# SSD decay factors on POOL and ACT alone, four factor buffers and the x weight pool at the other end of SBUF

## The chip, the cores and the metric

One core of a Trainium2 chip (trn2) runs the whole program. The metric is the device time of one execution, in microseconds (us). Before the change it is 1627.95 us, the median of three runs (1626.01 to 1629.65).

## The reference, cut to what matters

The network has a first block of two layers and a second block of two: an attention layer and a state-space (SSD) layer, each with a gated feed-forward. It works on 256 tokens of width 1024, with a context of 256 tokens beside them. The change lies in the SSD layer: 32 heads in 8 groups of 4, two chunks of 128 tokens, both directions. Per chunk and direction the reference computes

```
cum = cumsum(dt * A)
decay = exp(where(tri, cum[..., :, None] - cum[..., None, :], -inf))
cb = einsum('bcign,bcjgn->bcgij', Cc, Bc)
y_diag = einsum('bcghij,bcjghp->bcighp', cb[:, :, :, None] * decay, xdt)
```

with `xdt = x * dt`. For each head the kernel therefore needs a 128x128 matrix of factors, `decay * dt`, for the forward and for the backward direction (a lower and an upper triangle), and multiplies it by C and B's product, which is one for a group.

## The kernel before, in words

The dense layers run in fp32 in three products: each weight tile of 128x1024 is fetched by SP (`fetch`, L170), split into a high part `h` on ACT (L181) and a rest `l` on DVE (L182; on POOL for a few), and TensorE adds high times high, low times high and high times low (all recorded at L132). The x weights have a pool of their own, `wx`: three buffers of `raw`, two of `h`, two of `l`. A second pool, `wc`, and a scratch pool, `cx`, serve the context; they stand at the right end of SBUF and are given up (`cst.close()`) before the SSD layer, whose pool `l1` grows into their place from the left.

`x_ssm` loops over the eight groups. A turn does this:

- `project(g)`: four feature tiles (B, C and two of x, for x and the context together, C for x alone) into the two accumulators `pcvx`; each is convolved along the tokens in `conv_silu` (L1254 on ACT, L1255 and L1257 on DVE, which frees the accumulator, then a tanh on ACT, L1259, and L1260 on DVE). Then the gate `sz` (L1313 on ACT, L1314 on DVE), transposes, weighted copies `xc`, and the state `h0` of the context, copied out by ACT (L1330).
- The product of C and B, `pcb`; transposes and weighted copies `xf`; the state `hn`. Then for each chunk c: `GG` is the factor tile `EW[c]` times `pcb` (L1408, DVE), `pyd` its product with x on TensorE, `poff` the part of the earlier state; DVE sums them in `t` (L1417 to L1420) and gates them into `yg` (L1421); ACT squares it for the norm (L1422).
- `rstd`: a scalar step and a power on POOL (L288, L289); then `decays(g + 1)`; then ACT scales `yg` (L1428), TensorE transposes it into `pyt` (L1430), and it is split into `ysH` (ACT, L1434) and `ysL` (DVE, L1435).

`decays(g)` makes `EW` for both chunks, c = 0 and 1, 128x512 each (four heads). POOL makes two masks times dt, `W` and `Wb`, in one buffer each (L1361), and their sum (L1362). SP fetches the rows of cum, spread over all partitions, into `D_`, 128 partitions x 2 directions x 512, two buffers (L1364, 512 KB). POOL subtracts this token's cum from each direction (L1367, twice), DVE takes the min of both directions (L1368), ACT the exponential (L1370), POOL the product with W into `EW` (L1372), two buffers, one for each chunk.

Which order each engine's list has is settled before the run by the framework's planner, which lays the program out on a simulated timeline: an instruction written later may stand earlier in an engine's list if the planner expects it to be ready. On the chip each engine takes its list in order and waits at the head of it. SP's list holds all the weight and row fetches.

After the loop comes the out projection `ssm_w_out` (`pdx`), then the second feed-forward.

Of the kernel before, what the change touches and what calls it, by code (L numbers as in the profile page):

```python
# [8 lines left out]
F32 = mybir.dt.float32  # L9
F32R = mybir.dt.float32r  # L10
BF16 = mybir.dt.bfloat16
AF = mybir.ActivationFunctionType
ALU = mybir.AluOpType
# [12 lines left out]
CTAG = 's'  # L26
FINM = None
WB = 1
CWP = 1
WA = (0, 0)  # L30
DB = 2
XB = 2
PCB = 'cs'
# [4 lines left out]
PHS = 'cm'  # L38
PHX = 'cm'
POF = 'cd'  # L40
EB = 2
TAD = 'V'
LP = (4, 0, 2, 0, 2, 4)
ARAW = 2
# [3 lines left out]
WX = (3, 2)  # L48
WC = (2, 2)
# [42 lines left out]
def build(tc, A):  # L92
    nc = tc.nc
    T, V, S, G, SY = nc.tensor, nc.vector, nc.scalar, nc.gpsimd, nc.sync
    es = ExitStack()
# [5 lines left out]
    def dram(a, off, ap):  # L101
        return bass.AP(tensor=a.tensor, offset=a.offset + off, ap=ap)

    def pool(name, bufs=1, space=None, right=False):
        kw = {"side": "right"} if right else {}
        if space is not None:
            kw["space"] = space
        else:
            kw["reuse_waits"] = "tile"
        return tc.tile_pool(name=name, bufs=bufs, **kw)  # L110
# [5 lines left out]
    class Banks:  # L116
        def __init__(self, name, bufs):
            self.p = es.enter_context(pool(name, 1, PS))
            self.bufs = bufs
            self.k = name[2]  # L120
# [33 lines left out]
    flip = misc[:, 420:548]  # L154

    class Weights:
        def __init__(self, name, raw, hl, eng, right=False):
            self.p = (cst if right else es).enter_context(pool("w" + name, raw, right=right))
            self.hl = hl
            self.eng = eng  # L160

            self.ahead = []
            self.n = 0
            self.name = name
            self.on_pool = 0
# [21 lines left out]
    def cols(a, ncols, n0, k0=0, kt=8):  # L187
        return [(lambda t: t, dram(a, k0 * 128 * ncols + n0, [[ncols, 128], [128 * ncols, kt], [1, 128]]))]

    wx = Weights("x", *WX, SY)  # L190
    cst = ExitStack()
    wc = Weights("c", *WC, SY, right=True)
    cx = cst.enter_context(pool("cx", right=True))
    xw = es.enter_context(pool("xw"))
    xpool = {"x": (xw, "xn"), "c": (cx, "cfl")}
# [1066 lines left out]
    def heads(ap, n=4, d=64):  # L1262
        return ap[:, :, None].to_broadcast([128, n, d])
# [24 lines left out]
    def x_ssm():  # L1288
        with ExitStack() as st:
# [58 lines left out]
            wst = p.tile([128, 2, 32], F32, name="wst")  # L1348
            for c in range(2):
                V.tensor_tensor(wst[:, c], dec[:, 4 + c], dt[:, c, 32 * c:32 * c + 32], op=ALU.mult)  # L1350
            def decays(g):
                out = []
                for c in range(2):
                    W, Wb = (p.tile([128, 4, 128], F32, tag=n, bufs=WB, name=n) for n in ("W", "Wb"))
                    for d, msk, to in ((0, m_le, W), (1, m_ge, Wb)):
                        j = 32 * d + 4 * g
                        if WA[d]:
                            for h in range(4):
                                S.activation(to[:, h], msk, AF.Copy, scale=dt[:, c, j + h:j + h + 1])
                        else:  # L1360
                            G.tensor_tensor(to, msk[:, None, :].to_broadcast([128, 4, 128]), heads(dt[:, c, j:j + 4], 4, 128), op=ALU.mult)  # L1361
                    G.tensor_tensor(W, W, Wb, op=ALU.add)  # L1362
                    D_ = p.tile([128, 2, 4, 128], F32, tag="D_", bufs=DB, name="D_")
                    SY.dma_start(D_.rearrange("p d h i -> p d (h i)"),  # L1364
                                 dram(cum_s, (2 * c * 32 + 4 * g) * 128, [[0, 128], [32 * 128, 2], [1, 512]]))
                    for d in range(2):
                        G.tensor_tensor(D_[:, d], D_[:, d], heads(cum[:, 2 * c + d, 4 * g:4 * g + 4], 4, 128), op=ALU.subtract)  # L1367
                    V.tensor_tensor(D_[:, 0], D_[:, 0], D_[:, 1], op=ALU.min)  # L1368
                    E = D_[:, 0]
                    S.activation(E, E, AF.Exp)  # L1370
                    EW = p.tile([128, 4, 128], F32, tag="EW", bufs=EB, name="EW")
                    (G if CWP else V).tensor_tensor(EW, E, W, op=ALU.mult)  # L1372
                    out.append(EW)
                return out

            ew = decays(0)
            for g in range(8):
                h0, fT, fC, sz = project(g)
                h4 = slice(4 * g, 4 * g + 4)
                EW = ew  # L1380
                BT, CT = fT[:, 2, 0], fC[:, 0]
                xf = [p.tile([128, 3, 256], F32, tag="xf", bufs=XB, name="xf") for _ in range(2)]
                pcb = PT(PCB).tile([128, 2, 256], F32, tag=PCB[1], name="pcb")
                for c in range(2):
                    cs = slice(c * 128, (c + 1) * 128)
                    mm(pcb[:, c, 0:128], BT[:, cs], CT[:, cs], True, True)
                bt = p.tile([128, 2, 128], F32, tag="bt", bufs=2)
                for c in range(2):
                    cs = slice(c * 128, (c + 1) * 128)
                    pt = PT(PXT).tile([128, 512], F32, tag=PXT[1], name="pxt")  # L1390
                    for i in range(3):
                        T.transpose(pt[:, i * 128:(i + 1) * 128], fT[:, i, 0, cs], ident)
                    S.activation(bt[:, c], pt[:, 256:384], AF.Copy)
                    S.activation(xf[c][:, 0], pt[:, 0:256], AF.Copy)
                    for k, sc in ((2, wst[:, c, h4]), (1, d_row[:, h4])):
                        V.tensor_tensor(hview(xf[c][:, k]), hview(pt[:, 0:256]), heads(sc), op=ALU.mult)
                hn = p.tile([128, 2, 256], F32, tag="hn", bufs=2)
                ph = PT(PHX).tile([128, 2, 256], F32, tag=PHX[1], name="phx")
                for d in range(2):
                    mm(ph[:, d], bt[:, d], xf[d][:, 2], True, True)  # L1400
                    V.tensor_tensor(hview(hn[:, d]), hview(h0[:, d]), heads(dec[:, 6 + d, h4]), op=ALU.mult)
                V.tensor_tensor(hn, hn, ph, op=ALU.add)
                yg = p.tile([128, 2, 256], F32, tag="yg", bufs=2)
                ss = p.tile([128, 2], F32, tag="yss", bufs=2)
                for c in range(2):
                    cs = slice(c * 128, (c + 1) * 128)
                    GG = p.tile([128, 4, 128], F32, tag="GG", bufs=2)
                    V.tensor_tensor(GG, EW[c], pcb[:, c, None, 0:128].to_broadcast([128, 4, 128]), op=ALU.mult)  # L1408
                    py = PT(PYD).tile([128, 512], F32, tag=PYD[1], name="pyd")
                    for h in range(4):  # L1410
                        mm(py[:, h * 64:(h + 1) * 64], GG[:, h], xf[c][:, 0, h * 64:(h + 1) * 64], True, True)
                    po = PT(POF).tile([128, 2, 256], F32, tag=POF[1], name="poff")
                    mm(po[:, 0], CT[:, cs], h0[:, 0] if c == 0 else hn[:, 0], True, True)
                    mm(po[:, 1], CT[:, cs], h0[:, 1] if c == 1 else hn[:, 1], True, True)
                    t = p.tile([128, 2, 256], F32, tag="yt", bufs=1)
                    for d in range(2):
                        V.tensor_tensor(hview(t[:, d]), hview(po[:, d]), heads(dec[:, 2 * c + d, h4]), op=ALU.mult)  # L1417
                    (V if TAD == "V" else G).tensor_tensor(t[:, 0], t[:, 0], t[:, 1], op=ALU.add)
                    (V if TAD == "V" else G).tensor_tensor(t[:, 0], t[:, 0], xf[c][:, 1], op=ALU.add)
                    V.tensor_tensor(t[:, 0], t[:, 0], py[:, 0:256], op=ALU.add)  # L1420
                    V.tensor_tensor(yg[:, c], t[:, 0], sz[:, c], op=ALU.mult)  # L1421
                    S.activation(t[:, 1], yg[:, c], AF.Square, accum_out=ss[:, c:c + 1])  # L1422
                r = rstd(ss, 1024, 2, "y")
                if g < 7:
                    ew = decays(g + 1)
                pt = PT(PYT).tile([128, 2, 2, 128], F32, tag=PYT[1], name="pyt")
                for c in range(2):
                    S.activation(yg[:, c], yg[:, c], AF.Copy, scale=r[:, c:c + 1])  # L1428
                    for k in range(2):
                        T.transpose(pt[:, k, c], yg[:, c, k * 128:(k + 1) * 128], ident)  # L1430
                for k in range(2):
                    kk_ = 2 * g + k
                    pk = pt[:, k].rearrange("p c t -> p (c t)")
                    S.activation(yH[:, kk_], pk, AF.Identity, scale=g_ssm[:, kk_:kk_ + 1])  # L1434
                    V.scalar_tensor_tensor(yL[:, kk_], pk, g_ssm[:, kk_:kk_ + 1], yH[:, kk_].bitcast(F32),  # L1435
                                           op0=ALU.mult, op1=ALU.subtract)
# [71 lines left out]
```

## Time and profile before

| | us |
|---|---|
| three runs | 1626.01, 1627.95, 1629.65 |
| the profiled execution, its own time | 1627.45 |
| its span, first to last instruction | 1625.4 |
| TensorE (PE) busy | 1524.9 |
| VectorE (DVE) busy | 1104.7 |
| ScalarE (ACT) busy | 745.3 |
| GpSimd (POOL) busy | 301.8 |
| loop over the groups, first `sz` of group 0 to first `sz` of group 7 | 1091.0 to 1361.0 |

A span is cut into windows by the reader; a window's line gives each engine's busy time in it, the mean granted clock of TensorE (1.00 is full speed) and the share of its DMA engines that moved data. Rows of the timeline are single instructions: start, length, engine, line of the kernel, and in brackets how long the engine was idle before it and what ended that. The chain of waits follows the end of the program back to what released each step; rows of it are start, length and what. A tile's name may carry a number (`D__12148`): one allocation of it.

### The profile page before, as it was taken

What the parts mean: (1) busy time and instruction counts of PE and PEld (TensorE: products, weight loads), DVE (VectorE), ACT (ScalarE), POOL (GpSimd) and SP (SyncE); (2) the same over time, 40 slices, a digit from 0 to 9 for tenths busy, and PEclk for the clock granted to TensorE, in tenths of its full rate; (3) what the DMA queues carried; (4) which work ended last, traced back from release to release, by engine and by line L of the source; (5) the groups of instructions that cost most, each with busy time, mean ns of one, the idle gap of its engine ahead of it and who ended that gap; (6) DMA issues with size and microseconds to landing.
All of it is one profiled execution on the core that took longest, in us unless ns stands there. A gap on an engine that the chain in (4) does not pass through costs nothing.

```text
span 1625.4 us, 27122 instructions
## 1 busy us (share of the span) xinstructions
PE 1524.9 (94%) x10660; PEld 1307.0 (80%) x10660; DVE 1104.7 (68%) x1823; ACT 745.3 (46%) x1336; POOL 301.8 (19%) x260
## 2 busy tenths in 40 slices
PE   6989987999999999999999999887999999899998
PEld 5655664786998988888889897787899889699997
DVE  6789776567766676655666565569888787655666
ACT  3412256545544544666444343433454444444443
POOL 4476420000100100000000000129454430100000
PEclk9989998999999999999999999889999999999999
DMA  8755574466656656423665766334444433555664
GB/s 264 216 183 170 167 202 138 124 179 209 185 178 205 197 175 194 138 79 95 200 206 183 235 185 204 99 90 131 106 119 117 113 97 114 162 162 176 192 185 136
DMA packets 302735, 264.58 MB, mean 163 GB/s; under 512 B 27329, under 2 KB 256495, under 8 KB 302608
## 3 DMA queue, kind: packets, MB, share of 16 engines
q1 hardware_dynamic: 301680, 259.70, 53.5%
q0 software_dynamic: 928, 3.15, 0.7%
q8 instruction: 84, 1.38, 0.3%
q14 instruction: 43, 0.35, 0.1%
HBM read 261.47 MB, written 1.34 MB: 162 GB/s over the span
## 4 chain that ended last, share of the span: by engine, by line
PE 77%; DVE 7%; DMA 7%; POOL 5%; issue 2%; ACT 1%; SPq 1%; POOLq 0%; DVEq 0%; ACTq 0%
PE pdx L132 21%; PE pffnx L132 16%; PE pffnc L132 8%; PE pdc L132 7%; PE pcvx L132 6%; PE pada L905 3%; DMA araw<-ada_w 2%; PE pg L132 2%; PE py L132 2%; PE pl0x L132 1%; POOL EW L1372 1%; PE pl1x L132 1%; PE pocx L132 1%; PE ptcx L1086 1%; DVE l L182 1%
## 5 line engine op out<-in xcount | busy, mean ns | idle before, releaser
L182 DVE TENSOR_TENSOR l<-raw,h 128x1024 fp32r<-128x1024 f32 (+2 forms) x362 | 452.9, 1254 | 284.8 <-ACT h L181 231.1
L181 ACT ACTIVATE h<-raw 128x1024 fp32r<-128x1024 f32 (+2 forms) x374 | 389.2, 1042 | 487.3 <-PE pdx L132 147.5
L132 PE MATMUL pffnx<-nhx,h 128*128 128x256 f32 x704 | 174.9, 286 | 0.0
L132 PE MATMUL pffnx<-nlx,h 128*128 128x256 f32 x704 | 174.7, 285 | 0.2 <-DVE nlx L352 0.2
L132 PEld LDWEIGHTS pffnx<-nhx,h 128*128 128x128 f32 x704 | 136.5, 194 | 1.2 <-issue 1.2
L132 PEld LDWEIGHTS pffnx<-nlx,h 128*128 128x128 f32 x704 | 136.3, 194 | 1.0 <-DVE nlx L352 0.9
L310 POOL TENSOR_TENSOR sums<-sums,nhalf 128x1 f32<-128x1 f32 x20 | 14.6, 730 | 559.0 <-DVE sums L306 542.0
L132 PE MATMUL pffnx<-nhx,l 128*128 128x256 f32 x704 | 99.0, 283 | 0.0
L905 PE MATMUL pada<-araw,cT 128*32 128x256 f32 x704 | 76.3, 403 | 18.5 <-DMA araw<-ada_w 18.5
L132 PEld LDWEIGHTS pffnx<-nhx,l 128*128 128x128 f32 x704 | 91.1, 193 | 0.0
L132 PE MATMUL pffnc<-nhc,h 128*128 128x256 f32 x352 | 87.1, 285 | 0.0
L132 PE MATMUL pcvx<-nhx,h 128*128 128x256 f32 x256 | 77.3, 309 | 9.3 <-DVE cv L1257 9.3
L182 POOL TENSOR_TENSOR l<-raw,h 128x1024 fp32r<-128x1024 f32 (+1 forms) x12 | 27.3, 2277 | 315.7 <-PE pdx L132 202.2
L132 PE MATMUL pffnc<-nlc,h 128*128 128x256 f32 x352 | 85.5, 281 | 0.0
L132 PE MATMUL pdx<-h,nhx 128*128 128x256 f32 (+1 forms) x256 | 83.6, 345 | 0.4 <-DVE cv L1257 0.4
L132 PE MATMUL pdx<-h,nlx 128*128 128x256 f32 (+1 forms) x256 | 80.7, 334 | 0.0
L132 PE MATMUL pdx<-h,fh 128*128 128x256 f32 (+1 forms) x264 | 78.8, 323 | 0.0
L132 PE MATMUL pdx<-h,fl 128*128 128x256 f32 (+1 forms) x264 | 77.8, 319 | 0.0
L132 PE MATMUL pcvx<-nlx,h 128*128 128x256 f32 x256 | 75.3, 302 | 0.0
L132 PEld LDWEIGHTS pffnc<-nhc,h 128*128 128x128 f32 x352 | 66.4, 189 | 2.8 <-issue 1.2
L132 PEld LDWEIGHTS pffnc<-nlc,h 128*128 128x128 f32 x352 | 66.4, 189 | 0.8 <-DVE ss L408 0.4
L132 PEld LDWEIGHTS pcvx<-nhx,h 128*128 128x128 f32 x256 | 51.8, 203 | 13.3 <-issue 13.1
(600 smaller groups left out, 3892.4 us busy)
## 6 DMA issues: line engine op xcount, KB each, us to landing
araw<-ada_w SPq DMA_DIRECT2D x88, 512.0 KB
raw<-ffn_w_gate SPq DMA_DIRECT2D x66, 512.0 KB
raw<-ffn_w_up SPq DMA_DIRECT2D x66, 512.0 KB
raw<-ffn_w_down SPq DMA_DIRECT2D x54, 512.0 KB
raw<-ssm_w_in SPq DMA_DIRECT2D x48, 512.0 KB
raw<-od_w_in SPq DMA_DIRECT2D x25, 512.0 KB
raw<-attn_w_qkv SPq DMA_DIRECT2D x24, 512.0 KB
raw<-attn_w_o SPq DMA_DIRECT2D x32, 256.0 KB
```

Of the source, the lines that this page charges most:

```text
L132: i = T.matmul(out, l, r, start=start, stop=stop)
L181: S.activation(h[:, :n], raw[:, :n], AF.Copy)
L182: (G if self.on_pool > 0 else V).tensor_tensor(l[:, :n], raw[:, :n], h[:, :n].bitcast(F32), op=ALU.subtract)
L310: G.tensor_tensor(s[:, 3:4], s[:, j - 1:j], nhalf[:, 0:1], op=ALU.pow)
L905: T.matmul(pt[32 * q:32 * q + 32, 0:256], cT[:, k, :], raw[:, q * 256:(q + 1) * 256], start=k == 0, stop=k == 7, tile_position=(0, 32 * q))
L1086: T.transpose(pt[:, e, r], P[:, e, r, ki * 128:(ki + 1) * 128], ident)
L1372: (G if CWP else V).tensor_tensor(EW, E, W, op=ALU.mult)
```

## The change

The x weight pool is taken from the right end of SBUF, before the context's pools, instead of from the left. `decays` is split: `decay_rows(g)` fetches the rows, and `decays(g, rows)` works on them. The rows of g + 1 are fetched at the head of turn g, and `decays(g + 1)` stands behind `project(g)` instead of behind the norm of turn g. The two subtractions become one over both directions, from a copy of cum in another order (`negc`, four small DVE copies). DVE's min goes: ACT takes a Relu of the negated difference, POOL adds both directions, ACT takes exp of minus the sum (one of the two directions is always 0). The masks, the product and their order on POOL stay otherwise. `EW` has four buffers instead of two. Two switches that had one setting are gone.

```diff
-EB = 2
+EB = 4
...
-            self.p = (cst if right else es).enter_context(pool("w" + name, raw, right=right))
+            self.p = stack.enter_context(pool("w" + name, raw, right=True))
...
-    wx = Weights("x", *WX, SY)
     cst = ExitStack()
-    wc = Weights("c", *WC, SY, right=True)
+    wx = Weights("x", *WX, SY, es)
+    wc = Weights("c", *WC, SY, cst)
...
-            def decays(g):
+            def decay_rows(g):
                 out = []
                 for c in range(2):
+                    D_ = p.tile([128, 2, 4, 128], F32, tag="D_", bufs=DB, name="D_")
+                    SY.dma_start(D_.rearrange("p d h i -> p d (h i)"),
+                                 dram(cum_s, (2 * c * 32 + 4 * g) * 128, [[0, 128], [32 * 128, 2], [1, 512]]))
+                    out.append(D_)
+                return out
+
+            def decays(g, rows_):
+                out = []
+                for c in range(2):
+                    D_ = rows_[c]
+                    G.tensor_tensor(D_.rearrange("p d h i -> p (d h) i"), D_.rearrange("p d h i -> p (d h) i"),
+                                    negc[:, c, g, :, None].to_broadcast([128, 8, 128]), op=ALU.subtract)
+                    S.activation(D_, D_, AF.Relu, scale=-1.0)
                     W, Wb = (p.tile([128, 4, 128], F32, tag=n, bufs=WB, name=n) for n in ("W", "Wb"))
...
                     G.tensor_tensor(W, W, Wb, op=ALU.add)
-                    D_ = p.tile([128, 2, 4, 128], F32, tag="D_", bufs=DB, name="D_")
-                    SY.dma_start(D_.rearrange("p d h i -> p d (h i)"),
-                                 dram(cum_s, (2 * c * 32 + 4 * g) * 128, [[0, 128], [32 * 128, 2], [1, 512]]))
-                    for d in range(2):
-                        G.tensor_tensor(D_[:, d], D_[:, d], heads(cum[:, 2 * c + d, 4 * g:4 * g + 4], 4, 128), op=ALU.subtract)
-                    V.tensor_tensor(D_[:, 0], D_[:, 0], D_[:, 1], op=ALU.min)
                     E = D_[:, 0]
-                    S.activation(E, E, AF.Exp)
+                    G.tensor_tensor(E, E, D_[:, 1], op=ALU.add)
+                    S.activation(E, E, AF.Exp, scale=-1.0)
                     EW = p.tile([128, 4, 128], F32, tag="EW", bufs=EB, name="EW")
-                    (G if CWP else V).tensor_tensor(EW, E, W, op=ALU.mult)
+                    G.tensor_tensor(EW, E, W, op=ALU.mult)
                     out.append(EW)
                 return out
 
-            ew = decays(0)
+            negc = p.tile([128, 2, 8, 8], F32, name="cumg")
+            for c in range(2):
+                for d in range(2):
+                    V.tensor_copy(negc[:, c, :, 4 * d:4 * d + 4], cum[:, 2 * c + d].rearrange("p (g h) -> p g h", h=4))
+            ew = decays(0, decay_rows(0))
             for g in range(8):
+                nrow = decay_rows(g + 1) if g < 7 else None
                 h0, fT, fC, sz = project(g)
                 h4 = slice(4 * g, 4 * g + 4)
                 EW = ew
+                if g < 7:
+                    ew = decays(g + 1, nrow)
...
                 r = rstd(ss, 1024, 2, "y")
-                if g < 7:
-                    ew = decays(g + 1)
```

## Rows read from the trace of the kernel before

**Rows 1.** The page's first part: busy us, share of the span, instructions.

```profile
PE 1524.9 (94%) x10660; PEld 1307.0 (80%) x10660; DVE 1104.7 (68%) x1823; ACT 745.3 (46%) x1336; POOL 301.8 (19%) x260
```

**Rows 2.** Windows, turns 1 to 4 and 7: length, PE, PEld, DVE, ACT, POOL, clock, DMA, GB/s.

```profile
1091.00:1137.80 46.80, 37.97 (x267) 34.90 (x266) 41.57 (x53) 18.51 (x35) 39.36 (x31) 0.93 0.50 138
1137.80:1178.00 40.20, 37.09 (x281) 35.62 (x280) 32.49 (x52) 18.37 (x37) 18.31 (x16) 0.96 0.42 107
1178.00:1214.60 36.60, 34.31 (x270) 32.72 (x269) 30.43 (x51) 17.37 (x34) 16.52 (x15) 1.00 0.45 116
1214.60:1252.70 38.10, 35.80 (x270) 34.21 (x270) 30.45 (x50) 17.37 (x34) 16.61 (x15) 0.96 0.40 111
...
1327.40:1361.00 33.60, 33.60 (x266) 32.33 (x266) 26.63 (x49) 16.13 (x31) 6.31 (x5) 1.00 0.31 95
```

**Rows 3.** PE's waits, 1091 to 1361: us in total, times, longest.

```profile
PE pcvx L132 <- DVE cv L1257: 9.3, 4, 2.4
PE phx L132 <- ACT h L1330: 3.1, 1, 3.1
```

**Rows 4.** The chain of waits, turns 2 to 4: start, us, what.

```profile
1157.39 5.08 PE pcvx L132 x30
...
1183.44 5.59 DMA D__12148<-cum_s
...
1189.10 2.09 POOL D__12148 L1367 x2
...
1191.21 1.74 DVE D__12148 L1368
...
1195.28 3.94 PE pcvx L132 x31
...
1231.91 5.43 PE pcvx L132 x31
```

**Rows 5.** The chain of waits in turn 1.

```profile
1117.62 1.30 DVE D__10894 L1368
...
1129.30 1.45 DVE D__11299 L1368
...
1134.68 0.60 DVE D__11312 L1368
```

**Rows 6.** DVE's timeline: start, us, engine, line, operation, tiles.

```profile
1100.34 1.73 DVE L1368 TENSOR_TENSOR D__10487<-D__10487 128x512 f32<-128x512 f32 x1 [0.60 <-POOL D__10487 L1367]
...
1128.02 1.28 DVE L1418 TENSOR_TENSOR t<-t 128x256 f32<-128x256 f32 x1
...
1163.73 0.43 DVE L1418 TENSOR_TENSOR t<-t 128x256 f32<-128x256 f32 x1
```

**Rows 7.** POOL's timeline, turns 1 and 4.

```profile
1104.39 1.28 POOL L1372 TENSOR_TENSOR EW<-D__10487,W 128x512 f32<-128x512 f32 x1
...
1134.18 0.55 POOL L288 TENSOR_SCALAR t<-ss 128x2 f32<-128x2 f32 x1 [2.31 <-ACT t L1422]
1134.82 1.37 POOL L1361 TENSOR_TENSOR Wb<-misc,dta 128x512 f32<-128x512 f32 x1
1136.15 0.70 POOL L289 TENSOR_TENSOR r<-t,nhalf 128x2 f32<-128x2 f32 x1
...
1217.89 2.16 POOL L1372 TENSOR_TENSOR EW<-D__12148,W 128x512 f32<-128x512 f32 x1
```

**Rows 8.** POOL's waits, 1143 to 1326.

```profile
POOL t L288 <- ACT t L1422: 79.6, 5, 16.7
```

**Rows 9.** ACT: a group of instructions, a wait and a table load.

```profile
L181 ACT ACTIVATE h<-raw 128x1024 fp32r<-128x1024 f32 x42 | 44.3, 1054 | 34.2 <-PE pcvx L132 24.2 <-DVE xc L1324 6.3 <-PE pdx L132 3.7
...
ACT D__12148 L1370 <- DVE D__12148 L1368: 3.2, 1, 3.2
...
50.72 1.28 ACT L419 ACT_TABLE_LOAD   x1
```

**Rows 10.** SP's queue, its waits, 1091 to 1361.

```profile
SPq L1364 <- POOL EW L1372: 41.1, 14, 3.9
```

More of the change, by code (lines that the diff above doesn't have):

```diff
@@ L28 @@
 WB = 1
-CWP = 1
-WA = (0, 0)
 DB = 2
@@ L156, in build, with __init__ @@
     class Weights:
-        def __init__(self, name, raw, hl, eng, right=False):
-            self.p = (cst if right else es).enter_context(pool("w" + name, raw, right=right))
+        def __init__(self, name, raw, hl, eng, stack):
+            self.p = stack.enter_context(pool("w" + name, raw, right=True))
             self.hl = hl
@@ L1356, in decays @@
                         j = 32 * d + 4 * g
[L1357 to L1361, printed above, removed]
-                    G.tensor_tensor(W, W, Wb, op=ALU.add)
-                    D_ = p.tile([128, 2, 4, 128], F32, tag="D_", bufs=DB, name="D_")
-                    SY.dma_start(D_.rearrange("p d h i -> p d (h i)"),
-                                 dram(cum_s, (2 * c * 32 + 4 * g) * 128, [[0, 128], [32 * 128, 2], [1, 512]]))
-                    for d in range(2):
-                        G.tensor_tensor(D_[:, d], D_[:, d], heads(cum[:, 2 * c + d, 4 * g:4 * g + 4], 4, 128), op=ALU.subtract)
-                    V.tensor_tensor(D_[:, 0], D_[:, 0], D_[:, 1], op=ALU.min)
+                        G.tensor_tensor(to, msk[:, None, :].to_broadcast([128, 4, 128]), heads(dt[:, c, j:j + 4], 4, 128), op=ALU.mult)
+                    G.tensor_tensor(W, W, Wb, op=ALU.add)
                     E = D_[:, 0]
-                    S.activation(E, E, AF.Exp)
+                    G.tensor_tensor(E, E, D_[:, 1], op=ALU.add)
+                    S.activation(E, E, AF.Exp, scale=-1.0)
                     EW = p.tile([128, 4, 128], F32, tag="EW", bufs=EB, name="EW")
-                    (G if CWP else V).tensor_tensor(EW, E, W, op=ALU.mult)
+                    G.tensor_tensor(EW, E, W, op=ALU.mult)
                     out.append(EW)
                 return out
-            ew = decays(0)
+            negc = p.tile([128, 2, 8, 8], F32, name="cumg")
[3 more added lines that the diff above has]
+            ew = decays(0, decay_rows(0))
             for g in range(8):
+                nrow = decay_rows(g + 1) if g < 7 else None
                 h0, fT, fC, sz = project(g)
```

## The prediction

> **What bounds the kernel now.** The page's first part comes first: TensorE is busy for 94% of the span and VectorE for 68% [rows 1], so a saving on another engine shows only where TensorE waits for it. The change lies in the loop over the eight groups of the SSD layer, so the second view is a table of windows, one for each turn of that loop, from the first VectorE operation on `sz` of the turn before to its own [rows 2]. Turn 7, 1327.4 to 1361, only finishes the last factors (POOL 6.31 us): its TensorE is busy all of its 33.60 us, at full granted clock, with VectorE at 26.63. It is the floor of a turn. Turns 1 to 6 take 46.8, 40.2, 36.6, 38.1, 38.1 and 36.6 us (of the four alike, two stand in the rows). Above six floors that is 13.2 + 6.6 + 3.0 + 4.5 + 4.5 + 3.0 = 34.8 us, the most that any change to the decays can win here.
>
> The third view is who TensorE waits for in these turns [rows 3]: four times, 9.3 us in total, for the convolution's L1257 on VectorE, and once, 3.1 us, for `h0`, which ScalarE copies out. The chain of waits tells why [rows 4]: the row transfer lands after 5.59 us, POOL subtracts, VectorE takes the min (1.74 us), and only behind that min in VectorE's list stand the convolution's operations that free TensorE's accumulator. So VectorE is held from 1191.21 on by an operation whose result goes into a product at 1217.89 [rows 7]. After such an idle stretch the same 31 matmuls take 5.43 instead of 3.94 us in two of the four turns [rows 4], where the granted clock is 0.96 instead of 1.00 [rows 2]: part of the stretch ran at the lower of the clock's two levels, 1.2 GHz. Turn 1 differs: VectorE is busy 41.57 of 46.80 us and POOL 39.36 [rows 2], and the chain runs through VectorE, three mins with 1.30, 1.45 and 0.60 us among it [rows 5].
>
> **The change, part by part.** *The min leaves VectorE.* Turns 3 to 6 lose the waits, 9.3 us, and two slow stretches of 5.43 - 3.94 = 1.5 each, in all 12.3. I take 10, since ScalarE gets new waits (below); the bounds are 0 and 15.0 (3.0 + 4.5 + 4.5 + 3.0). Turn 2 lost 3.1 to `h0` and 5.08 - 3.94 = 1.1 to the clock, 4.2; but `h0` stood on ScalarE behind the Exp, which waited for VectorE's min, and the Exp will wait for POOL instead, so I take 2, with 0 and 6.6 as ends. In turn 1 the chain loses 1.30 + 1.45 + 0.60 = 3.35 and, ahead of `xc`, a min of 1.73 with 0.60 of waiting before it [rows 6], in all 5.7; the first factors come a little later (next point), so I take 5, between 0 and 13.2.
>
> *POOL gets an add* of 128x512 for each half of a group, 16 in all. No row is this add; its like, the product into EW, took 1.28 and 2.16 in two of its rows [rows 7], so two adds are 2.6 to 4.3 us a turn on top of 16.5 busy [rows 2]. The two subtractions become one of the same elements, at no gain. At 19 to 21 busy of 34, POOL has room; its present slack is the 15 to 16 us that it stands before the norm's scalar operation [rows 8]. If that is gone, the norm is late (third rival). For the first group alone the add lies on the way to GG: one add and one Relu, against the min that goes: some 1 us, counted above.
>
> *ScalarE gets a Relu* of 128x1024, like the weight copy's 1.05 us [rows 9], 2.1 a turn on 17.37 busy of 36.6 [rows 2]. Relu brings no reload of its function table that the trace would lead one to expect: the last of three loads in the run is at 50.72 us [rows 9], and line 783's Relu lies between stages with Exp and Tanh long after it. More than its length counts its place: it waits for POOL's subtraction, and the Exp for POOL's add. Behind a waiting ScalarE stand weight copies and the convolution's first step. Today its wait for the Exp is 3.2 us in the second half of a turn [rows 9] and, in turns 3 to 6, it holds TensorE up only through VectorE. Bounds: no loss, or all that turns 2 to 6 win.
>
> *Rows fetched earlier.* The planner already runs ahead of the program's order: the rows that land at 1189 [rows 4] go into the product at 1217.89 [rows 7]. What holds the 16 fetches is the free buffer: SP waited 41.1 us in 14 stops for the product into EW [rows 10], 2.9 each, with weight fetches behind. This stays, since `D_` keeps two buffers; only now the fetches stand ahead of their turn's weight fetches in the program. I count nothing: TensorE's largest waits in the loop are for VectorE and ScalarE, none for a transfer [rows 3], which says that three raw weight buffers cover it. Without that cover the price is up to 2.9 us a turn.
>
> *Four EW buffers* let POOL go on before GG is done. POOL's product is then no longer tied to GG of the turn before, but it was a full turn early already: nothing, unless it moves the burst. *Four small copies* into `negc` run once, on VectorE, each below the 0.43 us of a 128x256 add [rows 6]: 1.7 at most, beside the 5.59 of the first transfer. *The x weight pool* changes addresses alone: left pools slide down by its 28 KB per partition, and the context pools by the same, so the same tiles lie over one another save for 4.5 KB more at the end of the layer's pool. Nothing, either way; a wait for an old tile there would show as a late first EW, not in the later turns.
>
> **The sum.** 10 + 2 + 5 = 17 us. The profiled execution took 1627.45 us, 1625.4 of it span; it lies 0.5 below the median of 1627.95. From the median: **1611**. The loop is followed by the out projection and the feed-forward, which the change leaves as they are.
>
> **Here a rule speaks against it.** VectorE's 128x256 add took 0.43 us alone and 1.28 beside a working POOL [rows 6], 0.85 more. The Trainium skill's "Perfetto Trace Analysis", section "Optimizing Scalar/DVE Operations", says that GpSimd and VectorE share a read port, so that moving operations between the two may not help. The rows bear out that they hold each other up. What this would do to the sum is the second rival.
>
> **The rivals.** *First, ScalarE takes over the wait* (chance 0.15). Four of its operations a turn then hang on POOL, in place of two on VectorE. If the convolution's first step or the weight copy stands behind them, TensorE's 2.3 us a turn stay. For it: waits of 3.2, and turn 2, where this did reach TensorE. Against it: in turns 3 to 6 it did not. Only turn 1's 5 us remain: 1623, between 1620 and 1628.
>
> *Second, POOL's adds give half of it back through VectorE* (0.12). Two adds stretch two VectorE operations by 0.85 each, 1.7 a turn, over four turns 6.8 on the convolution's path: 17 - 7 = 10, so 1618. For it: the stretched rows. Against it: VectorE loses more than that, 30.43 - 26.63 = 3.8 us of work a turn [rows 2].
>
> *Third, slower: the norm's scalar operations wait behind the burst on POOL* (0.11). Line 288's scalar step and line 289's power must get through POOL's list before ScalarE scales `yg` and TensorE transposes it, in order. In turn 1, where POOL was busy throughout, a 1.37-us mask product already came between the two [rows 7]. If the planner puts half a burst there (a subtraction of 2.1, two masks of 1.3, two adds and a product of 1.7, so 9.8 us), three turns make 29, of which TensorE covers a part with the matmuls ahead of the transposes; with 8 a turn it is 24, and 1611 + 24 = 1635. It decides as soon as POOL's slack before line 288, 79.6 us over five turns [rows 8], is eaten up; 3 to 4 of each 15 to 16 us are.
>
> That the change does little of what it says holds for the earlier fetch, and is in the forecast at nothing.
>
> **How the numbers follow.** The forecast has 0.62. Its own range: the low end takes turns 2 to 6 whole (4.2 + 12.3) and 9.5 of turn 1's 13.2: 26, so 1602; at the upper end, half of 17 gives 1619. The range of 1602 to 1626 also holds the second rival and most of the first; it leaves out the third and a little below. About 0.2%, 3.3 us, is what a measurement of this kernel tells from no change. Faster: 0.60 of the forecast, 0.11 of the second and 0.08 of the first, 0.79. Same: 0.02, 0.01 and 0.06, 0.09. Slower: 0.12.
>
> **What would show it.** Right: the turns of 36.6 to 40.2 come to 34 to 36 at a granted clock of 1.00; the 9.3 us for L1257 are gone from TensorE's waits; VectorE is at about 27 a turn, POOL at 19 to 21; no TensorE wait for the transposes of `yg`. Wrong: a new TensorE wait behind ScalarE's Relu or Exp (first rival), the weight split and the convolution longer on VectorE with TensorE still idle before L1254's accumulator (second), POOL without idle time before line 288 (third), or turns before 1078 that moved, which nothing here would explain.

## The result, and the profile after

| | us |
|---|---|
| before, four runs beside it | 1628.05 median (1626.01 to 1629.65) |
| after, four runs | **1604.04** median (1600.78 to 1607.82) |
| ratio | 0.9854, 95% interval 0.9829 to 0.9879 |
| profiled execution after: own time, span | 1600.78, 1599.0 |

The change makes the kernel 24 us faster. The profiled execution lies 3.3 us below its median; that of before lay 0.6 below. First the page's busy times, which answer to [rows 1].

```profile
PE 1506.0 (94%) x10660; PEld 1284.8 (80%) x10660; DVE 1101.0 (69%) x1811; ACT 758.9 (47%) x1352; POOL 328.2 (21%) x260
```

TensorE has as many matmuls as before and is busy 18.9 us less. Nothing in the prediction would do that: it took waits away and two slow stretches of 1.5 us each. Next, the windows, cut like [rows 2] (length, PE, PEld, DVE, ACT, POOL, clock, DMA, GB/s): turns 1 to 7, and from the last turn's `sz` to the first matmul of the second feed-forward, which is the out projection.

```profile
1079.54:1123.30 43.76, 37.27 (x275) 34.54 (x274) 35.21 (x49) 21.37 (x37) 37.30 (x25) 0.96 0.54 145
1123.30:1164.10 40.80, 35.62 (x265) 32.85 (x264) 33.69 (x46) 22.16 (x38) 38.49 (x26) 0.95 0.50 133
1164.10:1199.84 35.74, 34.01 (x257) 32.18 (x257) 31.58 (x42) 19.72 (x36) 28.44 (x19) 0.96 0.42 119
1199.84:1235.06 35.22, 34.64 (x274) 32.80 (x274) 30.78 (x48) 19.52 (x36) 19.26 (x14) 1.00 0.46 120
1235.06:1269.86 34.80, 34.11 (x271) 32.27 (x270) 31.02 (x48) 19.08 (x36) 19.25 (x14) 1.00 0.44 122
1269.86:1302.53 32.67, 32.67 (x265) 31.40 (x264) 27.21 (x49) 15.65 (x31) 7.77 (x6) 1.00 0.35 98
1302.53:1335.91 33.38, 33.38 (x270) 32.11 (x269) 25.52 (x49) 16.26 (x31) 1.98 (x2) 1.00 0.30 95
1335.91:1405.80 69.89, 60.72 (x287) 48.33 (x286) 45.77 (x76) 31.36 (x58) 10.07 (x8) 0.95 0.45 143
```

The same last window of before:

```profile
1360.96:1427.20 66.24, 58.18 (x272) 47.12 (x271) 41.84 (x67) 29.36 (x51) 6.84 (x6) 0.95 0.47 151
```

Laid end to end, the two spans (1625.4 and 1599.0) differ so: up to the first `sz` -11.5 (1091.03 to 1079.54), the seven turns -13.6 (269.9 to 256.4), the out projection +3.7, the rest -5.0 (198.2 to 193.2): together -26.4. So 16.5 of it lie ahead of the loop and behind the out projection, in code that the change leaves as it is. And of the loop's 13.6, 3.7 come back in the window behind it, which has 15 matmuls more (287 against 272) and POOL's last product of factors: work slid past the mark with which I measured the loop.

TensorE's waits in the loop, as in [rows 3]:

```profile
PE pcvx L130 <- DVE cv L1255: 4.9, 2, 3.4
PE poff L130 <- DVE hn L1411: 2.9, 4, 1.0
PE pdx L130 <- DVE cv L1255: 2.2, 5, 1.0
PE pdx L130 <- DVE l L180: 1.9, 2, 1.6
...
PE phx L130 <- ACT h L1328: 0.6, 1, 0.6
```

The convolution's wait for `pcvx` (now L1255) goes from 9.3 in four to 4.9 in two: those of turns 3 to 6 are gone, and 3.4 and 1.4 are new, in turns 1 and 2. At `pdx` the same line now costs 2.2, where it was 0.4. `h0` goes from 3.1 to 0.6. In turns 4 and 5 the clock is 1.00 where it was 0.96; in turn 3 it is 0.96 where it was 1.00.

### The profile page after: what moved, and what is told of

It is laid out like the page before. It is cut to its first block, busy times and chain, and to the rows that moved or that the text cites. A ratio compares the mean times of both kernels' runs of the same rounds, so it can differ in the third digit from the quotient of the medians.

```text
span 1599.0 us, 27128 instructions
## 1 busy us (share of the span) xinstructions
PE 1506.0 (94%) x10660; PEld 1284.8 (80%) x10660; DVE 1101.0 (69%) x1811; ACT 758.9 (47%) x1352; POOL 328.2 (21%) x260
## 4 chain that ended last, share of the span: by engine, by line
PE 76%; POOL 7%; DMA 6%; DVE 5%; issue 2%; ACT 2%; SPq 1%; POOLq 0%; DVEq 0%; ACTq 0%
PE pdx L130 21%; PE pffnx L130 15%; PE pffnc L130 8%; PE pdc L130 7%; PE pcvx L130 4%; PE pada L903 3%; DMA araw<-ada_w 2%; PE pg L130 2%; PE py L130 2%; PE pl0x L130 1%; PE pl1x L130 1%; POOL EW L1374 1%; POOL W L1369 1%; PE pocx L130 1%; DVE l L180 1%
## 5 line engine op out<-in xcount | busy, mean ns | idle before, releaser
L130 PE MATMUL pffnx<-nlx,h 128*128 128x256 f32 x704 | 169.1, 281 | 0.8 <-DVE nlx L350 0.8
L130 PE MATMUL pffnx<-nhx,h 128*128 128x256 f32 x704 | 169.1, 280 | 0.0
L130 PEld LDWEIGHTS pffnx<-nlx,h 128*128 128x128 f32 x704 | 132.9, 189 | 1.9 <-DVE nlx L350 1.4
L130 PEld LDWEIGHTS pffnx<-nhx,h 128*128 128x128 f32 x704 | 133.0, 189 | 0.8 <-issue 0.8
L130 PE MATMUL pcvx<-nhx,h 128*128 128x256 f32 x256 | 73.8, 296 | 4.9 <-DVE cv L1255 4.9
L130 PE MATMUL pdx<-l,nhx 128*128 128x256 f32 (+1 forms) x256 | 57.4, 337 | 1.9 <-DVE l L180 1.9
```

The source lines that it names most:

```text
L130: i = T.matmul(out, l, r, start=start, stop=stop)
```

## The experiments

My theory after the result was that the place of the weights in SBUF sets TensorE's pace, and the rival that the kernels before the loop differ by chance; the later runs ask which property of the place it is, and which part of the loop's change wins. They ran in four batches, each on one chip with the kernel before beside it (its medians: 1629.0, 1627.6, 1627.4 and 1628.7); differences are against that median.

### First: the parts alone

**The move alone.** The kernel before with the line `wx = Weights("x", *WX, SY, es)` moved behind `cst` and `pool(..., right=True)`.

> The kernel before with only the x weight pool moved to the right end; every engine's list stays as it was. Theory A (the place of the weights in SBUF sets TensorE's pace: the trace after is 11.5 us ahead before the loop and gains 5.4 more in the last feed-forward, with the same lists there): 1611 to 1619 us, matmuls of the feed-forward at 280 to 281 ns in place of 285. Theory B (those 17 us are chance of one profiled run): 1626 to 1630, 285 ns.

1614.34 us, ratio 0.9914 (0.9901 to 0.9927): -14.7 with all five engines' lists unchanged. The part that I costed at nothing is the larger one.

**All but the move.** The kernel after, with the x weights back at the left.

> The changed kernel with the x weight pool back at the left; lists as in the changed kernel. Theory A: 1615 to 1620, the loop's gain of about 10 alone, feed-forward matmuls at 285 ns. Theory B: 1602 to 1606, as the whole change.

1621.29 us, 0.9953 (0.9941 to 0.9966): -7.7. The two parts add up to -22.4, nearly the whole.

**The min back on VectorE**, the rest as after:

```diff
-                    S.activation(D_, D_, AF.Relu, scale=-1.0)
...
-                    G.tensor_tensor(E, E, D_[:, 1], op=ALU.add)
-                    S.activation(E, E, AF.Exp, scale=-1.0)
+                    V.tensor_tensor(E, E, D_[:, 1], op=ALU.min)
+                    S.activation(E, E, AF.Exp)
```

> The changed kernel with the min on VectorE and a plain Exp, in place of Relu, add and Exp of minus the sum; rows ahead, four EW buffers and the pool's place stay. If the min in VectorE's list is what the loop gains from: 1611 to 1616, with TensorE's waits for the convolution's last step back at 2 us a turn. If the earlier rows and the buffers are: 1602 to 1607.

1619.85 us, 0.9939 (0.9926 to 0.9951): above both expectations, and by its median 5.5 slower than the move alone. With the min on VectorE nothing is left of the loop's gain, though the rows come earlier, `EW` has four buffers and one subtraction does for two. TensorE now waits 8.4 us for `h0`, whose copy stands on ScalarE behind the Exp. That the min costs more here than in its old place is not shown: in the profiled runs the seven turns take 272.5 us, against 271.0 with the move alone.

```profile
PE phx L130 <- ACT h L1328: 8.4, 3, 3.1
PE pcvx L130 <- DVE cv L1255: 3.9, 3, 1.9
```

**Two factor buffers** (`EB = 2`), the rest as after.

> The changed kernel with two EW buffers. If the buffers are worth nothing, as predicted: 1602 to 1607. If POOL's product waiting for GG matters once the program asks for the factors before GG: 1608 to 1620, POOL's waits for GG in the list again.

1606.73 us, 0.9863 (0.9848 to 0.9878); the interval overlaps that of after. The sum hides two movements. With four buffers POOL runs on through turn 2 (busy 38.49 us above); with two its product waits for `GG`, and the turn has 28.04:

```profile
1127.30:1164.68 37.38, 33.63 (x264) 31.50 (x263) 30.27 (x45) 20.70 (x37) 28.04 (x18) 1.00 0.43 117
...
1199.09:1236.42 37.33, 36.10 (x276) 34.46 (x275) 30.96 (x49) 19.93 (x38) 20.18 (x14) 0.95 0.42 119
```

So four buffers make turn 2 longer by 3.4 us (40.80 against 37.38) and turn 4 shorter by 2.1, and over all seven turns 0.7 shorter. What POOL does to VectorE in turn 2 is read from the sums into `t`, here after with four buffers (start, us):

```profile
1160.93 1.13 DVE L1427 TENSOR_TENSOR t<-t 128x256 f32<-128x256 f32 x1
1162.10 1.15 DVE L1428 TENSOR_TENSOR t<-t,xf 128x256 f32<-128x256 f32 x1
...
1163.77 0.41 DVE L1429 TENSOR_TENSOR t<-t,pyd 128x256 f32<-128x256 f32 x1
```

and the same with two, where POOL stands idle at that time:

```profile
1162.90 0.41 DVE L1427 TENSOR_TENSOR t<-t 128x256 f32<-128x256 f32 x1
1163.35 0.42 DVE L1428 TENSOR_TENSOR t<-t,xf 128x256 f32<-128x256 f32 x1
...
1164.35 0.41 DVE L1429 TENSOR_TENSOR t<-t,pyd 128x256 f32<-128x256 f32 x1
```

L1427 and L1428, with both inputs in SBUF, are stretched from 0.4 to 1.1; L1429, one of whose inputs is an accumulator, is not. That is the rule of the Trainium skill's "SBUF — State Buffer", section "Who interferes with whom": a VectorE instruction with two SBUF inputs contends with a GpSimd instruction that reads SBUF.

### Second: which part of the loop's change, and what of the move

**The factors on POOL and ScalarE, in the old place**: pool at the right, `decays(g + 1)` behind the norm, rows fetched inside, two buffers, the four copies into `negc` ahead of the loop (not shown); against the move alone:

```diff
-                    for d in range(2):
-                        G.tensor_tensor(D_[:, d], D_[:, d], heads(cum[:, 2 * c + d, 4 * g:4 * g + 4], 4, 128), op=ALU.subtract)
-                    V.tensor_tensor(D_[:, 0], D_[:, 0], D_[:, 1], op=ALU.min)
+                    G.tensor_tensor(D_.rearrange("p d h i -> p (d h) i"), D_.rearrange("p d h i -> p (d h) i"),
+                                    negc[:, c, g, :, None].to_broadcast([128, 8, 128]), op=ALU.subtract)
+                    S.activation(D_, D_, AF.Relu, scale=-1.0)
                     E = D_[:, 0]
-                    S.activation(E, E, AF.Exp)
+                    G.tensor_tensor(E, E, D_[:, 1], op=ALU.add)
+                    S.activation(E, E, AF.Exp, scale=-1.0)
```

> The pool at the right, the factors on POOL and ACT, but made where the kernel before makes them: rows fetched inside, after the norm, two factor buffers. Theory A (the min's wait on VectorE was the loop's loss): the gain is whole without the earlier fetch, within 3 us of the run with two factor buffers (1606.7), so 1604 to 1610, and TensorE's wait for the convolution's L1257 is at most 2 us. Theory B (the earlier place of the rows and factors is what wins): the time stays by the run with the pool moved alone (1614.3), 1612 to 1618, with waits for the convolution near 9 us or new ones for ScalarE.

1604.02 us, 0.9862 (0.9847 to 0.9877): as after. Rows a group ahead, the earlier place and four buffers together are worth nothing that shows here. The new arithmetic is the loop's whole gain; and since the run with the min back on VectorE also has the single subtraction, and gains nothing, it is the min. In the profiled spans, 14.0 us apart, 11.8 lie in the seven turns and the out projection; 2.9 lie ahead of the loop, in code that this edit leaves as it is. The expected wait was missed: 3.2 us for `pcvx` and 4.7 for `pdx` stay, where I had said at most 2.

**64 unused bytes**, the kernel before with a pad ahead of the weights' pool at the left (and one behind it):

```diff
+    es.enter_context(pool("pa")).tile([128, 16], F32, name="pad")
     wx = Weights("x", *WX, SY)
+    es.enter_context(pool("pb")).tile([128, 16], F32, name="padb")
```

> The kernel before with 64 unused bytes a partition ahead of the x weight pool and 64 behind it: weights shifted by 64 bytes, all else on the left by 128, all five lists the same. Theory A (the region of SBUF counts): as before, 1627 to 1631, and 120 ns from one 128x256 matmul to the next in the first feed-forward. Theory B (the low bits of the weights' addresses count: in the changed kernel they are 64 bytes off from before, modulo 128): as the pool moved alone, 1612 to 1618, at 113 to 118 ns.

1612.04 us, 0.9907 (0.9885 to 0.9928): -15.6. Sixty-four bytes give what the move gave; the region of SBUF is not what counts.

**The weights' pool first of all**, at the left end, ahead of `con`.

> The kernel before with the x weight pool as the first pool at the left end, all resident pools 28 KB higher, layer pools where they were, all five lists the same. Theory A1 (the far, right part of SBUF is what helps, or the distance from the activations): as before or slower, 1627 to 1633, spacing 120 ns. Theory A2 (weights between the activations and the layers' pools are what hurts; either end is good): 1612 to 1620, spacing 113 to 118 ns. Theory B (the low bits): weights keep theirs modulo 128, so no change, 1627 to 1631.

1620.60 us, 0.9962 (0.9948 to 0.9976): -7.0, between all that was expected. My premise was wrong: the pool then begins at byte 16512, so the weights do not keep their low address bits; their distance from the activations becomes 96 modulo 128.

### Third: is it the address or the distance?

In the compiled program of before, the weights' `h` begins at byte 82336 of a partition and the activations `nhx` at 36512. The distance, 45824, is 0 modulo 128. After, it is 64. The same goes for the gated activations `fh` of the down projections (`pdx`) and the weights: 0 before, 64 after. The context's activations `nhc` stand at 64 from the context's weights in both.

**The activations shifted**: a pad of 64 bytes ahead of the pool `act`, 192 more ahead of the weights.

> The kernel before with 64 unused bytes a partition ahead of the activations' pool and 192 more ahead of the x weight pool: activations shifted by 64 bytes, weights and all that follows by 256, all five lists the same. Theory R (what counts is the distance of weights and activations modulo 128: 0 in the kernel before, 64 with the weights padded by 64, as here): 1608 to 1617 and a spacing of 113 to 118 ns. Theory W (the weights' own address modulo 128 counts, here as in the kernel before): 1626 to 1631 and 120 ns.

1621.51 us, 0.9954 (0.9938 to 0.9970): -5.9. Faster, so the weights' own address, unchanged modulo 128, does not decide alone; but only a part of what a distance of 64 gave before. The reason is in the other pairs: `fh` lies behind the weights and moves with them by 256 bytes, so the down projections stay at 0, and `nhc` moves with `nhx`, so the context's feed-forward goes from 64 to 0. The rows follow each pair (count, then busy us and mean ns of one). Before:

```profile
L132 PE MATMUL pffnx<-nhx,h 128*128 128x256 f32 x704 | 174.9, 286 | 0.0
L132 PE MATMUL pffnc<-nhc,h 128*128 128x256 f32 x352 | 87.1, 285 | 0.0
L132 PE MATMUL pdx<-h,fh 128*128 128x256 f32 x176 | 43.7, 285 | 0.0
```

With the activations shifted, `pffnx` is faster, `pffnc` slower and `pdx` as before:

```profile
L133 PE MATMUL pffnx<-nhx,h 128*128 128x256 f32 x704 | 171.3, 281 | 0.0
L133 PE MATMUL pffnc<-nhc,h 128*128 128x256 f32 x352 | 89.2, 288 | 0.0
L133 PE MATMUL pdx<-h,fh 128*128 128x256 f32 x176 | 43.7, 285 | 0.0
```

Worked out from the starts, the spacing in `pffnc` goes from 116 to 119 ns, and that of the down projection stays at 120. With the 64-byte pad above, where `fh` too is at 64 modulo 128, the last row has 42.4 us and 281 ns.

**Everything shifted**: a pad of 64 bytes ahead of `con`.

> The kernel before with 64 unused bytes ahead of all pools at the left: weights, activations and everything there shifted by 64 bytes alike, all five lists the same. Theory R (distance modulo 128): as before, 1626 to 1631 and 120 ns. Theory W (the weights' own address): 1608 to 1617 and 113 to 118 ns.

1629.71 us, 1.0017 (1.0004 to 1.0030): no gain, with the weights at the very address that gained 15.6 where the activations stayed. It is the **distance**. Only `nhc` comes from 64 to 0 here, and `pffnc` goes from 285 to 288 ns, which would account for the small loss.

**The kernel after with 32 unused bytes** at the right end ahead of the weights, so a distance of 32.

> The changed kernel with 32 unused bytes at the right end, so its weights begin on a multiple of 64 bytes and stand 32 instead of 64 bytes from the activations modulo 128; lists as in the changed kernel. If a start on 64 bytes is what helps: faster than the changed kernel's 1604, 1595 to 1602, spacing near 113 ns. If a distance of 64 is best (the first-pool run, at a distance of 96 modulo 128, gained only 7 us): slower, 1608 to 1614, spacing 118 ns throughout. If 32 and 64 are alike: 1602 to 1607.

1616.65 us, 0.9929 (0.9915 to 0.9944): about 12 us slower than after, though the weights now begin on a multiple of 64 bytes. The second of the three expectations has the sign and nearly the size.

### Fourth: the whole change without the move

**The kernel after, the weights at the left, with the 64-byte pads** of above.

> The changed kernel with the x weight pool back at the left end, and 64 unused bytes a partition ahead of and behind it. Theory R (all that the move gave is the 64 bytes of distance modulo 128 between weights and activations): as the changed kernel, 1601 to 1609. Theory S (the right end has a merit of its own beside the distance): 1612 to 1622, as without the pad.

1603.83 us, 0.9847 (0.9826 to 0.9869): as after. These 64 bytes give all that the move gave; the intervals leave no merit of the right end to be seen.

**The kernel after with 128 unused bytes** at the right end: the distance stays 64 modulo 128 and becomes 192 modulo 256.

> The changed kernel with 128 unused bytes at the right end: the weights' distance from the activations stays 64 modulo 128 and goes from 64 to 192 modulo 256. If 128 is the period that counts: 1601 to 1608, and the spacing goes between 113 and 118 ns. If 256 is the period (the run with the activations shifted stood at 192 and gained only 6 us, with 118 and 120 ns): 1609 to 1617 and 118 to 120 ns.

1608.24 us, 0.9864 (0.9840 to 0.9887). It stands between the two expectations, and its interval overlaps that of after: open.

All of it in one table. The distance is that of `h` from `nhx`. The spacing is that from the start of one 128x256 matmul to the next, worked out from the starts of the first feed-forward (in its first half, at full granted clock); PE is the page's busy time.

| kernel | loop | distance modulo 256 | spacing, ns | PE, us | median, us |
|---|---|---|---|---|---|
| before | old | 0 | 120 | 1524.9 | 1627 to 1629 |
| all shifted | old | 0 | 120 | 1531.9 | 1629.71 |
| pool first | old | 224 | 118 | 1518.9 | 1620.60 |
| activations shifted | old | 192 | 118 | 1519.0 | 1621.51 |
| move alone | old | 64 | 118 | 1511.6 | 1614.34 |
| 64-byte pad | old | 64 | 118 | 1512.4 | 1612.04 |
| min back on VectorE | new, min on VectorE | 64 | 113 | 1508.6 | 1619.85 |
| all but the move | new | 0 | 120 | 1528.4 | 1621.29 |
| 32 bytes | new | 32 | 118 | 1525.0 | 1616.65 |
| 128 bytes | new | 192 | 118 | 1515.3 | 1608.24 |
| after | new | 64 | 118 | 1506.0 | 1604.04 |
| two factor buffers | new | 64 | 113 | 1504.4 | 1606.73 |
| factors in the old place | new | 64 | 113 | 1505.3 | 1604.02 |
| left, 64-byte pad | new | 64 | 113 | 1502.7 | 1603.83 |

One stretch does not stand for a whole run, which goes over from 118 to 113 or back. Over all of `pffnx`, spacings below 150 ns alone, the mean is 120.0 in the three kernels at 0, 118.3 with 32 bytes, 117.8 with the activations shifted, 117.5 with the pool first, and 115.6 to 116.7 in the others.

The spacing can be seen in the timeline, in a block of eight matmuls (seven spacings and one duration of 0.28 us). Before:

```profile
869.65 1.12 PE L132 MATMUL pffnx<-nhx,l 128*128 128x256 f32 x8
```

Before with everything shifted, the distance as it was:

```profile
873.38 1.12 PE L133 MATMUL pffnx<-nhx,l 128*128 128x256 f32 x8
```

Before with the 64-byte pad:

```profile
869.80 1.10 PE L132 MATMUL pffnx<-nhx,l 128*128 128x256 f32 x8
```

And the kernel after with its weights at the left and the pad:

```profile
869.47 1.07 PE L130 MATMUL pffnx<-nhx,l 128*128 128x256 f32 x8
```

No version here beats the kernel after: the one with the old place of the factors (1604.02) and the one with the pad at the left (1603.83) equal it.

## Why the prediction was right, and where it was not

The time lies in the range, 7 us below the forecast, and the sign is right. But the number comes out of two terms that were wrong in opposite directions, so its nearness is luck: the loop's 17 us were 8 to 9, and some 15 came from a term put at nothing. The loop alone, at 1621.29 us, would also have stayed in the range.

**"The x weight pool changes addresses alone ... Nothing, either way."** This step failed, and it is the larger part of the result: -14.7 alone, with identical lists. I asked which tiles come to lie over one another, and not how the weights lie to the activations that TensorE reads in the same matmul. The prediction had named the sign to look for, turns before 1078 that moved; the first `sz` came 11.5 us earlier (6.1 with the move alone).

**"10 + 2 + 5 = 17 us" from the loop.** The runs that separate it give -7.7 (all but the move, against before) and some -9 (factors in the old place, against the move alone, each by its own chip's median: -23.6 and -14.7). Term by term, with the move left out:

- Turns 3 to 6: 10 forecast, 9.3 measured (149.6 to 140.3). Right, by the mechanism named: the waits of 2.3 us a turn for the convolution at `pcvx` are gone there, and the clock is 1.00 in turns 4 to 6. In turn 3 it fell, from 1.00 to 0.97, which the prediction did not have.
- Turn 1: 5 forecast, 3.2 measured (46.81 to 43.59). In after VectorE has 35.21 instead of 41.57 us of work in it, but POOL is at 37.30 of 43.76; what holds the rest is not separated.
- Turn 2: 2 forecast, a loss of 0.7 measured (40.12 to 40.83). The term was mis-signed for a reason that the prediction mentions and drops: four buffers are "nothing, unless it moves the burst". They do. POOL's work in turn 2 goes from 18.31 [rows 2] to 38.49 us, beside VectorE's. The trace of before had the sign: POOL's product stopped for `GG` (L1372 for L1408) six times in the loop, 15.5 us in all, and with four buffers not once.
- Behind the loop: nothing forecast, 3.7 us lost (66.24 to 69.91, 15 matmuls more), and 0.7 in turn 7. The turns were cut by `sz`, and a gain between two marks was taken for a gain of the whole. With the work that slid past the last mark, -11.1 in the turns is -7.5.

**Rows fetched earlier, at nothing**: right; the run without it is as fast. SP's stops for the free buffer stay too (39.8 us in 13, against [rows 10]). **Four buffers, at nothing**: right in the sum, by a loss in turn 2 and gains in turns 4 and 6. **Relu without a table load**: right; the last of three loads starts at 49.70 us.

**The rivals.** *ScalarE takes over the wait*: no. It waits for POOL up to 3.8 us at a Relu, but TensorE's wait for `h0` falls to 0.6. Such a wait shows with the min on VectorE and the factors moved (8.4 for `h0`), where the Exp ahead of the copy waits for VectorE. *POOL's adds give half back through VectorE*: true of the mechanism, in turn 2, as the rows of `t` show; over the whole loop the two-buffer run, where VectorE is spared it, is no faster. *Slower, the norm behind the burst*: it began to happen. In turn 3 two instructions of POOL came between the norm's own two steps (L286 and L287):

```profile
1169.34 1.14 POOL L286 TENSOR_SCALAR t<-ss 128x2 f32<-128x2 f32 x1
1170.56 1.04 POOL L1368 TENSOR_TENSOR Wb<-misc,dta 128x512 f32<-128x512 f32 x1
1171.56 1.29 POOL L1371 TENSOR_TENSOR D__11756<-D__11756 128x512 f32<-128x512 f32 x1
1172.80 0.72 POOL L287 TENSOR_TENSOR r<-t,nhalf 128x2 f32<-128x2 f32 x1
```

They are factor work, 2.3 us. It stayed small because POOL kept its slack before the norm, 68.0 us in four turns (79.6 in five, [rows 8]); ScalarE waited 4.4 us in four for `r`, TensorE not at all for the transposes.

**The rule that spoke against the change**: that POOL and VectorE hold each other up is borne out by the stretched rows (0.41 to 1.13 us), and it did not decide the time: both buffer counts give the same within their intervals.

## What to carry to other kernels

Where a change moves a pool, look at the distance in bytes between the operands that one matmul reads, and try a pad of 64 bytes before crediting the move or the rest of the change: here it was worth 15 us, for nothing else changed. Look at every pair, since a pad that helps one can put another at 0. Run each part of a change alone when they can add up by chance, as -15 and -8 did to a number not far from a forecast of -17 for the second part alone. And when gains are read between marks in a loop, read the window behind the last mark too.

## What the runs showed of the hardware that was not expected

TensorE's pace depends on where its two SBUF operands lie to each other. At a distance of 0 modulo 128 bytes, 128x256 fp32 matmuls with a new weight tile each start 120 ns apart, at full granted clock, in all three kernels that have it. At 64 they start 113 or 118 ns apart, at 32 and 96 about 118 (single spacings there scatter from 115 to 123). It goes by the pair and not by the kernel: with the activations shifted, `pffnx` is at 118 and, in the same run, `pdx` of the down projection, still at a distance of 0, at 120. Which of 113 and 118 comes is not set by the addresses: after and its two-buffer variant have the same lists and places up to the loop, and in the same stretch one runs at 118, the other at 113. What in the chip makes it so, no run here shows. The Trainium skill's "SBUF — State Buffer", section "Who interferes with whom", gives TensorE two independent read ports, one for the moving operand and one for weight loads, and says that it never waits on anyone; by that, the pads would have done nothing. They did 15 us, so for this kernel the measurement decides against it.

Three things stay open. What decides between 113 and 118 is one. The second is whether the period is 128 or 256 bytes: the kernel after with 128 more bytes is the one run that asks it of all pairs, and the interval of its 1608.24 us overlaps that of after. Against 256 speaks the pad at the left (1603.83): there `fh` stands at 192 modulo 256, where after has 64, and nothing is lost. The run with the activations shifted does not bear on it, since some of its pairs stand at 0. The third is which stages gained. Of the move's 10.2 us in the profiled spans, 6.1 lie before the first `sz` and 5.1 behind the out projection; in the seven turns, where TensorE also waits, its quicker pace gained nothing (+1.1). With the 64-byte pad the same lists gained 3.0 before the first `sz` and 3.2 in the turns, so single traces do not settle a stage: that first stretch, in which the lists differ at its end alone, takes 1079.1 to 1088.0 us in the eight traces with `nhx` and `fh` at 64 modulo 128, and 1091.0 to 1095.4 in the three with both at 0.
